# A hybrid transformer layer in split fp32: each stage's first pair of weights queued ahead of its last operands, and work moved between three engines

## Chip, cores and metric

The kernel runs on one core of one Trainium2 chip, in one launch. The metric is the device time of that launch in microseconds (us).

## What is computed

One layer on 1024 tokens of width 1024, all float32 (cut to what matters here):

```python
u = rmsnorm(h, g_mix_pre)
z = u @ w_in                          # 1024 x 4256; holds the two gates gate_a, gate_b
ya = (a_b * causal_dwconv3(a_c * a_x, conv_a_w)) @ w_a_out
yb = chunk_causal_attention(q, k, v) @ w_b_out
mixed = sigmoid(gate_a) * ya + sigmoid(gate_b) * yb
h = h + rmsnorm(mixed @ w_o, g_mix_post)
u2 = rmsnorm(h, g_ffn_pre)
up = causal_dwconv3(u2 @ w_ffn_up, conv_ffn_w) + b_ffn_conv    # width 2 x 2816
f = (gelu(up[:, :2816]) * up[:, 2816:]) @ w_ffn_down
h = h + rmsnorm(f, g_ffn_post)
h = h + rmsnorm((p @ w_ple_proj) * sigmoid(h @ w_ple_gate), g_ple_post)
```

## The kernel before

**Arithmetic.** Every fp32 operand is split into a high part (a cast on ScalarE, L181) and a low part (source minus high part, L182, on VectorE or GpSimd). A product is then three passes of matmuls. The large products are done on 2 x 2 blocks with seven block products in place of eight; one block product is 12 matmuls of 128x128 by 128x512 (`prod`, L300).

**Operands of a stage.** `x_blocks` turns eight activation tiles into seven operands: B11 and B21 (`first`), then B22, T2 and four wide subtractions of 128x2048 (`second`, L278), then T3, T1 and T4 (`third`). A `third` is released only once the last subtraction has been issued on VectorE.

**Weights.** `pair` turns two weight rows into two output rows. It loads both rows, forms S-combinations (two on GpSimd as a rule, L338 and L339; two on VectorE, L340 and L341), splits them, and runs the seven products. VectorE gathers them from PSUM (L348 to L363).

**First rows.** `first_row` does two of the seven products alone, those that need only B11 and B21. It runs for some pairs ahead of the stage, so that TensorE has work while the other operands are made. ScalarE copies the first product out of PSUM (L313), VectorE adds the second to it (L319); in the last stage GpSimd and VectorE add both to what is there (L316, L317). Such a pair is *early* and needs five products later.

**Order.** Each engine has an instruction queue that it works off in order. The queues' order is fixed when the kernel is built, by a scheduler that places instructions by modelled times; the source's order, tile buffers (rings of slots, `raws` for raw weight rows) and explicit `issue_after` edges bound it.

**Stages.** TensorE takes up new operands four times: at the gates (about 60 to 140 us into the span; 6 first rows), at the FFN's up projection (about 765 to 860 us; 12 first rows, with the layer's merge, its two norms and the residual add before it), and at two groups of the down projection (1200 to 1240 us and 1280 to 1340 us; 4 first rows each). In the merge, each half h computes a norm, eight residual adds (L845, L846), a second norm and the scaled activations (L852). A norm's sum over channels is made of squares (ScalarE, L247), summed on VectorE (L250), then by tiny matmuls with ones (L228) and transposes (L240) on TensorE. Between up and down the gated product of the FFN (`gated`: the convolution L513, gelu L891, a multiplication L892) goes to DRAM (`d_f`) and comes back as the operands of down.

## Time and profile before

| | us |
|---|---|
| median of 3 runs | 1546.74 (1546.2, 1546.74, 1549.32) |
| the profiled execution's own time | 1545.98 |
| its span in the trace | 1544.1 |
| TensorE busy in the span | 1476.6 (96%) |
| VectorE busy | 1174.8 (76%) |
| ScalarE busy | 689.0 (45%) |
| GpSimd busy | 545.0 (35%) |

The profile calls TensorE's matmuls PE, its weight loads PEld, VectorE DVE, ScalarE ACT, GpSimd POOL, and the queue that issues most DMAs SP. PEclk is the clock that TensorE was granted, as a share of full speed. Numbers after L are lines of the kernel before, where the text does not say otherwise.

### The profile page before, as it was taken

The page shows a single profiled execution, that of the slowest core. Times are in us where ns is not written, and L with a number is a line of the kernel's source. Part 1 is how long each engine was busy: PE and PEld are TensorE (multiplying, and loading weights), DVE is VectorE, ACT ScalarE, POOL GpSimd, SP SyncE. Part 2 cuts the span into 40 slices and gives each one's busy share as a digit, 9 for nine tenths or more (in the row PEclk, how much of TensorE's full clock was granted, in tenths as well). Part 3 has the DMA queues.
Part 4 walks back from the last instruction along what each step waited for, and adds up shares of the span by engine and source line. Part 5 has one row for each costly group of instructions (what it writes and reads, how often), then busy time and mean ns, then how long its engine had stood idle before and what let it go on. Part 6 is the DMA issues. An engine that isn't in the chain of part 4 may idle for free. (4 is left out here: it accounts for less than half of the span.)

```text
span 1544.1 us, 19277 instructions
## 1 busy us (share of the span) xinstructions
PE 1476.6 (96%) x6980; PEld 1225.9 (79%) x6980; DVE 1174.8 (76%) x1663; ACT 689.0 (45%) x1082; POOL 545.0 (35%) x402
## 2 busy tenths in 40 slices
PE   8999999999989999999998999999999699899996
PEld 6777888888778888888886888888888577688796
DVE  6897666665568888845579988889889878647876
ACT  8534222334457777343344444444446234135433
POOL 1333222226333343431033332223330214756963
PEclk9999999999999999999999999999999899999998
DMA  9344221336741013633271233334325523353332
GB/s 346 120 150 156 82 82 55 123 124 231 253 132 49 31 42 110 206 108 100 106 272 42 95 110 125 121 123 137 100 92 191 177 69 118 93 170 110 109 113 93
DMA packets 73503, 195.56 MB, mean 127 GB/s; under 512 B 7360, under 2 KB 22208, under 8 KB 73408
## 3 DMA queue, kind: packets, MB, share of 16 engines
q1 hardware_dynamic: 65056, 169.90, 33.6%
q10 hardware_dynamic: 8352, 24.44, 4.1%
q8 instruction: 55, 0.90, 0.2%
q14 instruction: 40, 0.33, 0.1%
HBM read 142.79 MB, written 51.51 MB: 126 GB/s over the span
## 5 line engine op out<-in xcount | busy, mean ns | idle before, releaser
L300 PE MATMUL psum<-s,s 128*128 128x512 f32 x3948 | 915.1, 393 | 32.7 <-DVE s L182 8.8
L300 PEld LDWEIGHTS psum<-s,s 128*128 128x128 f32 x3948 | 743.1, 189 | 199.6 <-DVE s L182 16.9
L181 ACT CAST s<-s 128x512 fp32r<-128x512 f32 (+3 forms) x431 | 340.1, 811 | 477.0 <-PE psum L300 157.6
L182 POOL TENSOR_TENSOR s<-s,s 128x512 fp32r<-128x512 f32 (+2 forms) x186 | 280.4, 1520 | 726.2 <-PE psum L300 423.7
L215 PE MATMUL psum<-s,s 128*128 128x512 f32 (+1 forms) x1920 | 413.4, 373 | 15.2 <-ACT s L181 13.5
L215 PEld LDWEIGHTS psum<-s,s 128*128 128x128 f32 x1920 | 335.6, 191 | 77.5 <-ACT s L181 15.5
L182 DVE TENSOR_TENSOR s<-s,s 128x1024 fp32r<-128x1024 f32 (+2 forms) x245 | 308.7, 1278 | 46.6 <-ACT s L181 44.2
L513 DVE SCALAR_TENSOR_TENSOR psum<-s,vecs,psum 128x1023 f32<-128x1023 f32 (+1 forms) x88 | 111.7, 1280 | 1.0
L250 DVE TENSOR_TENSOR s<-s,s 128x512 f32<-128x512 f32 (+1 forms) x83 | 65.9, 797 | 42.6 <-ACT s L247 40.6
L511 ACT ACTIVATE psum<-s,vecs 128x1024 f32<-128x1024 f32 x44 | 53.0, 1208 | 94.1 <-DVE s L359 80.6
L182 DVE TENSOR_TENSOR s<-psum,s 128x512 fp32r<-128x512 f32 (+3 forms) x144 | 70.8, 504 | 27.5 <-ACT s L181 26.3
L181 ACT CAST s<-psum 128x512 fp32r<-128x512 f32 (+3 forms) x144 | 61.2, 445 | 38.0 <-DVE s L182 13.9
L247 ACT ACTIVATE s<-s 128x512 f32<-128x512 f32 (+1 forms) x82 | 47.8, 590 | 52.8 <-DVE s L1004 21.3
L731 PE MATMUL psum<-s,s 128*128 128x512 f32 (+2 forms) x288 | 67.4, 360 | 2.3 <-ACT s L742 2.2
L338 POOL TENSOR_TENSOR s<-s 128x512 f32<-128x512 f32 x45 | 65.4, 1454 | 3.4
L339 POOL TENSOR_TENSOR s<-s,s 128x512 f32<-128x512 f32 x43 | 65.0, 1513 | 3.3
L744 POOL TENSOR_SCALAR s<-s,ri 128x384 f32<-128x384 f32 (+5 forms) x48 | 41.3, 861 | 70.3 <-DVE ri L743 52.8
L357 DVE TENSOR_TENSOR s<-s,psum 128x512 f32<-128x512 f32 x47 | 32.1, 683 | 34.0 <-PE psum L300 31.4
L756 PE MATMUL psum<-s,s 128*128 128x256 f32 x320 | 54.1, 292 | 1.5 <-DVE s L182 0.7
L731 PEld LDWEIGHTS psum<-s,s 128*128 128x128 f32 x288 | 46.4, 189 | 9.9 <-ACT s L742 5.3
L742 ACT ACTIVATE s<-psum,nm 128x128 f32<-128x128 f32 (+3 forms) x64 | 47.5, 745 | 14.3 <-DVE nm L740 8.9
L756 PEld LDWEIGHTS psum<-s,s 128*128 128x128 f32 x320 | 45.5, 189 | 6.0 <-DVE s L182 2.0
(115 smaller groups left out, 1067.2 us busy)
## 6 DMA issues: line engine op xcount, KB each, us to landing
s<-in_w_up_dram SPq DMA_DIRECT2D x56, 512.0 KB, 3.7
s<-in_w_in_dram SPq DMA_DIRECT2D x40, 512.0 KB, 3.8
s<-in_w_down_dram SPq DMA_DIRECT2D x36, 512.0 KB, 3.7
d_f<-s SPq DMA_DIRECT2D x22, 512.0 KB, 2.6
s<-in_x_dram SPq DMA_DIRECT2D x32, 256.0 KB, 5.4
d_sg<-s ACTq DMA_DIRECT2D x16, 512.0 KB, 3.1
s<-d_sg SPq DMA_DIRECT2D x16, 512.0 KB, 4.2
s<-d_f SPq DMA_DIRECT2D x16, 512.0 KB, 5.8
```

The lines of the kernel that those rows point to most:

```text
L181: A.copy(hi, src)
L182: (eng or V).tensor_sub(lo, src, f(hi))
L215: nc.tensor.matmul(out_ps, w[c // HALF][pw][:, c % HALF : c % HALF + P], X[k][half][px][:, cs], start=start and a == 0 and k == 0, stop=st ...
L247: A.activation(sq, src, AF.Square)
L250: V.tensor_add(acc, acc, sq)
L300: nc.tensor.matmul(pt, w[pw][:, k * P : (k + 1) * P], blk[k][px], start=a == 0 and k == 0, stop=a == 2 and k == 3,)
L338: who[2].tensor_add(a22, a21, a22)
L339: who[3].tensor_sub(a21, a11, a21)
L511: A.activation(dst, src, AF.Identity, bias=bias, scale=w2)
L513: V.scalar_tensor_tensor(dst[:, i:], src[:, : S - i], w, dst[:, i:], op0=ALU.mult, op1=ALU.add)
L731: nc.tensor.matmul(st_[:, lo_ : lo_ + w_], q[part_q][:, o : o + P], parts(K[hd, kh])[part_k][:, 0:w_], start=part_q == 0 and part_k == 0, ...
L756: nc.tensor.matmul(po[:, 0:256], vt[:, kt, :], t_[:, kk * 256 : (kk + 1) * 256], start=kt == 0 and part == 0, stop=kt == 2 * b + 1 and par ...
```

## The change

1. **First rows leave by ScalarE.** `first_row` copies the second product out of PSUM on ScalarE, where VectorE added it to the first. The sum of the two is made on GpSimd when the early pair starts.
2. **Weights apart from products.** The part of `pair` that loads and makes weights is now `weights`. At the gates, at up and at the first group of down, the weights of the first pair are issued ahead of `third`, and `third` waits for three things to be issued on VectorE: the last subtraction, T2 and the last split of those weights. In the second group of down they are issued ahead of `second`, and `third` does not wait for them. The rings of raw slots start at other slots, and have one slot more in the first group of down.
3. **Norm squares in PSUM.** In the merge the squares go to PSUM banks 5 and 6.
4. **Residual adds.** All 16 are on GpSimd (eight were).
5. **Down weights.** All on VectorE (18 operations were on GpSimd). The last group's low parts of the first half (6 splits) go from GpSimd to VectorE, and wait for the weights of the last two pairs.

```diff
     def square_sum(acc, src, accs, sqs):
-        sq = single(*(accs if acc is None else sqs)())[:, :n]
+        at = (accs if acc is None else sqs)()
+        sq = (single(*at) if isinstance(at, tuple) else bank(at))[:, :n]
...
         def second():
...
             operand("T2", 4, 1)
-            t4.append(sub(b21, b21, b22))
+            ends["sum"] = sub(b21, b21, b22)
-        def third():
-            with tc.issue_after(t4[0].ins):
+        def third(w=None):
+            with ExitStack() as after:
+                for i in (ends["sum"], ends["T2"], *([w["end"]] if w else [])):
+                    after.enter_context(tc.issue_after(i.ins))
                 operand("T3", 0, 1)
...
         if add:
-            G.tensor_add(d11, d11, m1)
             V.tensor_add(d11, d11, b2)
         else:
-            V.tensor_add(d11, b2, m1)
+            A.copy(d11, b2)
-    def pair(src0, src1, B, raws, banks, out0, out1, early=False, hooks=(), add=None, who=(V, G, G, G)):
+    def weights(src0, src1, raws, early=False, who=(V, G, G, G)):
...
+        w["S2"], w["S4"] = wide(r0, V)
+        w["S3"], w["S1"] = wide(r1, V)
+        w["end"] = last[-1]
+        return w
+    def pair(w, B, banks, out0, out1, hooks=(), add=None):
...
+        if "A11" in w:
+            A.copy(m1, times("A11", "B11"))
+            V.tensor_add(d11, times("A12", "B21"), m1)
+        else:
+            G.tensor_add(d11, d11, m1)
...
     second()
-    third()
+    w = gate_weights(spilled, True)
+    third(w)
...
-    sqs, accs, sqs2, accs2 = (Ring(singles(i)) for i in (46, 47, 48, 49))
+    sqs, accs, accs2 = Ring([5, 6]), Ring(singles(47)), Ring(singles(49))
-    sbk, rbk = Ring([4, 5, 6]), Ring([7])
+    sbk, rbk = Ring([4]), Ring([7])
...
-            (G if k % 2 else V).tensor_add(y, y, xr)
+            G.tensor_add(y, y, xr)
...
+    raws = Ring([42, 43, 7, 8])
+    mm = Ring(range(4))
+    w = up_weights(0)
     third()
-    raws = Ring([7, 8, 42, 43])
-    mm = Ring(range(4))
...
-        raws = Ring([7, 8] if g else [7, 8, 45])
+        raws = Ring([7, 8] if g else [7, 8, 45, 50])
...
+        def down_weights(i):
+            return weights(w_down[8 * g + 2 * i], w_down[8 * g + 2 * i + 1], raws, True, (V, V, V, V))
+        w = down_weights(0)
         second()
         if g == 0:
-            free = [50]
-            gated(*last)
-        third()
-        raws = Ring([7, 8, 22, 23] if g else [8, 45, 7, 50])
+            gated(*before, fo=before[2])
+        third(w if g == 0 else None)
+        raws = Ring([22, 23, 7, 8] if g else [45, 50, 7, 8])
...
-            split(raw, *fX[k][h], V if h else G)
+            with tc.issue_after(ends[2 + h]):
+                split(raw, *fX[k][h], V)
```

**VectorE's queue at the entry to up**, from the scaled activations of the second half on. In these rows sN is a tile in slot N; slots 7, 8, 42 and 43 hold raw weight rows, 34 to 41 the activations, 17, 21, 25, 29 and the split at 38 receive operands (T2 at 21 is made from 34; T3 and T1 at 25 and 29 from 38; T4 at 38 from 34), 0, 3 and 50 receive split weights. In the changed kernel L182 is L183, L278 is L281, L340 and L341 are L338 and L339, and L852 is L869. Before:

```order
L852 SCALAR_TENSOR_TENSOR s34_102<-s34_102,vecs_70,psum_69 128x512 x4
L278 TENSOR_TENSOR s38_2471<-s38_2471 128x4x512
L319 TENSOR_TENSOR s33_5883<-psum_69,s33_5883 128x512
L340 TENSOR_TENSOR s7_88<-s8_89,s7_88 128x512
L182 TENSOR_TENSOR s17_539<-s34_102,s17_539 128x2x512 x2
L278 TENSOR_TENSOR s38_2471<-s34_102,s38_2471 128x4x512
L319 TENSOR_TENSOR s46_4960<-psum_69,s46_4960 128x512
L341 TENSOR_TENSOR s7_88<-s7_88 128x512
L182 TENSOR_TENSOR s0_124<-s8_89,s6_422 128x1024
L278 TENSOR_TENSOR s34_102<-s34_102,s38_2471 128x4x512
L319 TENSOR_TENSOR s47_4961<-psum_69,s47_4961 128x512
L182 TENSOR_TENSOR s50_5853<-s7_88,s45_5852 128x1024
```

And now:

```order
L869 SCALAR_TENSOR_TENSOR s34_102<-s34_102,vecs_70,psum_69 128x512 x4
L183 TENSOR_TENSOR s2_134<-s7_88,s1_127 128x1024
L281 TENSOR_TENSOR s38_2477<-s38_2477 128x4x512
L183 TENSOR_TENSOR s17_539<-s34_102,s17_539 128x2x512 x2
L281 TENSOR_TENSOR s38_2477<-s34_102,s38_2477 128x4x512
L281 TENSOR_TENSOR s34_102<-s34_102,s38_2477 128x4x512
L338 TENSOR_TENSOR s42_4890<-s43_4891,s42_4890 128x512
L281 TENSOR_TENSOR s34_102<-s34_102 128x4x512
L339 TENSOR_TENSOR s42_4890<-s42_4890 128x512
L183 TENSOR_TENSOR s21_119<-s34_102,s21_119 128x2x512 x2
L183 TENSOR_TENSOR s25_564<-s38_2477,s25_564 128x2x512 x2
L183 TENSOR_TENSOR s29_569<-s38_2477,s29_569 128x2x512 x2
```

The three L319 adds are gone from between the subtractions. Behind the rows shown the queue now has the two weight splits (s0, s50) and the last operand (s38, two splits). Before, it had two operands (s25, s29), a gathering add, the operand at 21, the second pair's L340 and the last operand.

**VectorE's queue at the first group of down.** Slots 9 to 16 hold the activations, 45 and 50 raw weight rows, 34 and 49 outputs of first rows; T2 goes to slot 38, T3 to 17, T1 to 42, 43, 33 and 44. In the changed kernel L513 is L530, L892 is L914, and the GpSimd or VectorE weights L338 and L339 are L336 and L337. Before:

```order
L278 TENSOR_TENSOR s13_8423<-s13_8423 128x4x512
L182 TENSOR_TENSOR s17_539<-s9_8418,s17_539 128x2x512 x2
L182 TENSOR_TENSOR s42_8577<-s9_8418,s42_8577 128x512
L182 TENSOR_TENSOR s43_8578<-s9_8418,s43_8578 128x512
L182 TENSOR_TENSOR s33_8579<-s9_8418,s33_8579 128x512
L182 TENSOR_TENSOR s44_8580<-s9_8418,s44_8580 128x512
L182 TENSOR_TENSOR s38_6218<-s13_8423,s38_6218 128x2x512 x2
L513 SCALAR_TENSOR_TENSOR psum_69<-s48_4996,vecs_70,psum_69 128x1022
L338 TENSOR_TENSOR s45_8416<-s45_8416 128x512
L319 TENSOR_TENSOR s34_102<-psum_69,s34_102 128x512
L319 TENSOR_TENSOR s49_4997<-psum_69,s49_4997 128x512
```

And now:

```order
L281 TENSOR_TENSOR s13_8441<-s13_8441 128x4x512
L183 TENSOR_TENSOR s38_6238<-s13_8441,s38_6238 128x2x512
L530 SCALAR_TENSOR_TENSOR psum_69<-s48_5002,vecs_70,psum_69 128x1022
L183 TENSOR_TENSOR s38_6238<-s13_8441,s38_6238 128x2x512
L337 TENSOR_TENSOR s8_89<-s7_88,s8_89 128x512
L183 TENSOR_TENSOR s5_4885<-s50_8435,s5_4885 128x512
L914 TENSOR_TENSOR s46_4966<-s46_4966,psum_69 128x1024
L338 TENSOR_TENSOR s7_88<-s8_89,s7_88 128x512
L336 TENSOR_TENSOR s50_8435<-s50_8435 128x512
L183 TENSOR_TENSOR s4_389<-s8_89,s3_137 128x1024
L183 TENSOR_TENSOR s17_539<-s9_8436,s17_539 128x2x512 x2
```

The adds that emptied two first rows' banks stood behind eight operand splits and a convolution; now no such add is in the queue, and T2 is split first, and the first pair's weights (raw slots 7 and 8) stand ahead of the splits of T3 and T1.

**GpSimd's queue in the merge.** The residual adds of one half; the last weights of the merge stand ahead. Slots 42 and 43 hold the halves of x. Before:

```order
L182 TENSOR_TENSOR s33_356<-s7_88,s33_356 128x512
L846 TENSOR_TENSOR s38_2471<-s38_2471,s42_4884 128x512
L846 TENSOR_TENSOR s38_2471<-s38_2471,s43_4885 128x512
L846 TENSOR_TENSOR s34_102<-s34_102,s42_4884 128x512
L846 TENSOR_TENSOR s34_102<-s34_102,s43_4885 128x512
```

And now:

```order
L183 TENSOR_TENSOR s33_356<-s7_88,s33_356 128x512
L863 TENSOR_TENSOR s38_2477<-s38_2477,s42_4890 128x512 x2
L863 TENSOR_TENSOR s38_2477<-s38_2477,s43_4891 128x512 x2
L863 TENSOR_TENSOR s34_102<-s34_102,s42_4890 128x512 x2
L863 TENSOR_TENSOR s34_102<-s34_102,s43_4891 128x512 x2
```

Four adds of a half became eight in a row on the same engine.

## Rows read from the trace of the kernel before

**Rows 1.** The page's head: busy time, share of the span and count of instructions of TensorE (with its weight loads), VectorE, ScalarE and GpSimd.

```profile
PE 1476.6 (96%) x6980; PEld 1225.9 (79%) x6980; DVE 1174.8 (76%) x1663; ACT 689.0 (45%) x1082; POOL 545.0 (35%) x402
```

**Rows 2.** Windows by stage (gates, entry to up, rest of up, down's first group, down's second group, what follows): start and end, then their length, busy us (and instructions) of PE, PEld, DVE, ACT, POOL, the granted clock, the DMA share and GB/s.

```profile
60.00:140.00 80.00, 74.88 (x316) 58.12 (x315) 71.79 (x102) 37.37 (x49) 29.57 (x17) 1.00 0.39 134
820.00:860.00 40.00, 34.65 (x133) 25.31 (x132) 38.17 (x35) 14.82 (x17) 19.52 (x10) 0.91 0.16 53
860.00:1180.00 320.00, 320.00 (x1413) 265.15 (x1413) 287.38 (x312) 139.08 (x143) 92.47 (x63) 1.00 0.37 123
1200.00:1240.00 40.00, 27.56 (x102) 20.99 (x102) 35.68 (x37) 12.09 (x13) 11.48 (x6) 0.87 0.47 166
1280.00:1340.00 60.00, 50.21 (x209) 39.68 (x209) 48.27 (x42) 18.09 (x25) 36.33 (x24) 0.94 0.40 123
1340.00:1400.00 60.00, 60.00 (x267) 49.68 (x266) 34.52 (x47) 20.65 (x34) 35.81 (x27) 1.00 0.43 140
```

**Rows 3.** Waits over the whole span: engine, tile and line that waited, what it waited for, total us, times, longest us.

```profile
PE psum L300 <- DVE s L182: 8.8, 12, 1.8
PE psum L300 <- DVE s L319: 6.7, 1, 6.7
PE psum L300 <- DVE s L350: 6.4, 1, 6.4
PE psum L300 <- DVE s L349: 6.1, 2, 5.2
...
DVE s L340 <- POOL s L339: 18.7, 14, 4.4
```

**Rows 4.** Instructions by source line: count, then shortest, median and longest duration in ns, first and last start.

```profile
L278 DVE TENSOR_TENSOR s<-s x8: 2282/2292/3384, 56.4 to 1280.9; 128x2048 f32<-128x2048 f32 x8
...
L340 DVE TENSOR_TENSOR s<-s,s x45: 677/685/1780, 55.8 to 1324.4; 128x512 f32<-128x512 f32 x45
...
L319 DVE TENSOR_TENSOR s<-psum,s x22: 682/688/698, 46.0 to 1210.6; 128x512 f32<-128x512 f32 x22
...
L313 ACT COPY s<-psum x26: 567/586/592, 43.4 to 1299.0; 128x512 f32<-128x512 f32 x26
...
L339 POOL TENSOR_TENSOR s<-s,s x43: 1274/1294/3219, 50.1 to 1322.1; 128x512 f32<-128x512 f32 x43
...
L846 POOL TENSOR_TENSOR s<-s,s x8: 1285/1300/3589, 720.0 to 782.2; 128x512 f32<-128x512 f32 x8
```

**Rows 5.** Timeline at the gates, first PE, then VectorE: start, length, engine, line, operation, count, and in brackets idle time before it and what ended it.

```profile
54.81 19.20 PE L300 MATMUL psum<-s,s 128*128 128x512 f32 x84
74.83 0.73 PE L300 MATMUL psum<-s,s 128*128 128x512 f32 x2 [0.82 <-ACT s L181]
...
72.79 0.69 DVE L340 TENSOR_TENSOR s<-s,s 128x512 f32<-128x512 f32 x1 [1.18 <-POOL s L339]
```

**Rows 6.** Timeline at the entry to up, PE, then VectorE.

```profile
804.58 25.43 PE L300 MATMUL psum<-s,s 128*128 128x512 f32 x111
830.45 0.73 PE L300 MATMUL psum<-s,s 128*128 128x512 f32 x2 [0.43 <-DVE s L182]
...
841.72 8.52 PE L300 MATMUL psum<-s,s 128*128 128x512 f32 x24 [1.49 <-DVE s L182]
...
804.86 5.35 DVE L852 SCALAR_TENSOR_TENSOR s<-s,vecs,psum 128x512 f32<-128x512 f32 x8 [1.73 <-PE psum L240]
...
824.79 3.37 DVE L278 TENSOR_TENSOR s<-s 128x2048 f32<-128x2048 f32 x1
828.09 5.71 DVE L182 TENSOR_TENSOR s<-s,s 128x1024 fp32r<-128x1024 f32 x4
```

**Rows 7.** Timeline of the second half's two norms, PE between the first norm's transposes (at 771.07) and the second norm's sum, then GpSimd's residual adds.

```profile
771.42 24.07 PE L300 MATMUL psum<-s,s 128*128 128x512 f32 x105
795.34 0.95 PE L228 MATMUL psum<-ones,s 128*128 128x1 f32 x8
...
773.65 2.60 POOL L846 TENSOR_TENSOR s<-s,s 128x512 f32<-128x512 f32 x2 [43.81 <-DVE s L845]
779.52 4.92 POOL L846 TENSOR_TENSOR s<-s,s 128x512 f32<-128x512 f32 x2 [3.27 <-DMA s<-in_x_dram]
```

**Rows 8.** Timeline at down's first group: PE, VectorE, ScalarE.

```profile
1211.42 13.13 PE L300 MATMUL psum<-s,s 128*128 128x512 f32 x48 [6.67 <-DVE s L319]
1229.76 7.33 PE L300 MATMUL psum<-s,s 128*128 128x512 f32 x24 [5.22 <-DVE s L349]
...
1201.23 7.04 DVE L182 TENSOR_TENSOR s<-s,s 128x1024 fp32r<-128x1024 f32 x8
1208.18 1.29 DVE L513 SCALAR_TENSOR_TENSOR psum<-s,vecs,psum 128x1022 f32<-128x1022 f32 x1
...
1209.97 1.30 DVE L319 TENSOR_TENSOR s<-psum,s 128x512 f32<-128x512 f32 x2
...
1217.50 2.00 ACT L181 CAST s<-s 128x1024 fp32r<-128x1024 f32 x2 [2.28 <-DMA s<-d_f]
```

**Rows 9.** Timeline at down's second group: PE, then VectorE.

```profile
1321.57 15.45 PE L300 MATMUL psum<-s,s 128*128 128x512 f32 x60 [6.44 <-DVE s L350]
...
1313.32 1.76 DVE L340 TENSOR_TENSOR s<-s 128x512 f32<-128x512 f32 x1 [2.43 <-POOL s L339]
...
1320.82 0.69 DVE L350 TENSOR_TENSOR s<-psum,s 128x512 f32<-128x512 f32 x1
```

More of the change, by code (lines that the diff above doesn't have):

```diff
@@ L341, in pair, with times @@
         V.tensor_sub(a12, a12, a11)
[L342 to L343 removed]
+        w["S2"], w["S4"] = wide(r0, V)
[3 more added lines that the diff above has]
+    def pair(w, B, banks, out0, out1, hooks=(), add=None):
+        d11, d12, d21, d22 = out0[:, hs(0)], out0[:, hs(1)], out1[:, hs(0)], out1[:, hs(1)]
+        def times(a, b):
+            pt = bank(banks())
+            prod(pt, w[a], B[b])
+            return pt
         m1, u3 = (d12, d21) if add is None else add
         u2 = m1
[L346 to L350 removed]
+        if "A11" in w:
[3 more added lines that the diff above has]
+            G.tensor_add(d11, d11, m1)
+        V.tensor_add(u2, times("S2", "T2"), m1)
+        V.tensor_add(u3, times("S3", "T3"), u2)
         if add is not None:
@@ L353, in pair @@
                 G.tensor_add(d, d, u_)
-        pt = times(S1, "T1")
+        pt = times("S1", "T1")
         for hook in hooks[:1]:
@@ L358, in pair @@
         V.tensor_add(d12, d12, pt)
-        V.tensor_add(d21, d21, times(A22, "T4"))
-        pt = times(S4, "B22")
+        V.tensor_add(d21, d21, times("A22", "T4"))
+        pt = times("S4", "B22")
         for hook in hooks[1:]:
@@ L430, with gate_weights, gate_pair @@
     wblk.become([*range(NBLK), 33, 50])
-    def gate_pair(i, o, o2, early=False, hooks=()):
-        pair(w_in[17 + 2 * i], w_in[18 + 2 * i], B, raws, mm, f32(o), f32(o2), early, hooks)
+    def gate_weights(i, early=False):
+        return weights(w_in[17 + 2 * i], w_in[18 + 2 * i], raws, early)
+    def gate_pair(i, o, o2, early=False, hooks=(), w=None):
+        pair(w or gate_weights(i, early), B, mm, f32(o), f32(o2), hooks)
         for j, o_ in enumerate((o, o2)):
@@ L519 @@
             ct = 2 * g + j
-            pair(w_in[4 + ct], w_in[8 + ct], B, raws, mm, v, e)
+            pair(weights(w_in[4 + ct], w_in[8 + ct], raws), B, mm, v, e)
             V.tensor_mul(v, v, e)
@@ L524 @@
             rotary_tables()
-        pair(w_in[2 * g], w_in[2 * g + 1], B, raws, mm, v, e)
+        pair(weights(w_in[2 * g], w_in[2 * g + 1], raws), B, mm, v, e)
         for j, z in ((1, e), (0, v)):
@@ L537 @@
             w1 = w_in[12 + k1] if k1 < 5 else w_in[33]
-            pair(w_in[12 + k0], w1, B, raws, mm, f32(o[0]), f32(o[1]))
+            pair(weights(w_in[12 + k0], w1, raws), B, mm, f32(o[0]), f32(o[1]))
             for k, o_ in zip((k0, k1), o):
@@ L880, in up, with gated @@
         z1 = free.pop(0)
-        pair(w_up[j], w_up[NFF + j], B, raws, mm, f32(z0), f32(z1), j in early or j in spilled, who=(G, G, G, G))
+        pair(w, B, mm, f32(z0), f32(z1))
         return j, z0, z1
-    def gated(j, z0, z1):
+    def gated(j, z0, z1, fo=None):
         cv = []
@@ L894, in gated @@
         free.extend([z0, z1, fo])
-    last = up(0)
+    before = up(0, w)
     for j in range(1, NFF):
-        now = up(j)
-        gated(*last)
-        last = now
+        now = up(j, up_weights(j))
+        gated(*before)
+        before = now
     raws = Ring([7, 8])
@@ L906 @@
     free = [i for i in free if i not in extra]
-    yacc = [i for two in zip(free[:4], [*free[4:], *last[1:]]) for i in two]
+    yacc = [i for two in zip(free[:4], [*free[4:], *before[1:]]) for i in two]
     extra = [42, 43, *extra]
```

46 lines of the change are left out of this document (20 added, 26 removed).

## The prediction

> **What bounds the kernel now.** I read the page's head first: TensorE is busy 96% of the span, every other engine far less [rows 1]. So time can only be won where TensorE stands or runs slowly. The windows by stage show where. In the long part of up TensorE never stands: 1413 matmuls in 320 us, 0.2265 us each [rows 2]. With that as yardstick, each stage's window minus its matmuls at 0.2265 is what the stage loses: gates 80 − 316 × 0.2265 = 8.4 us; entry to up 40 − 133 × 0.2265 = 9.9; down's first group 40 − 102 × 0.2265 = 16.9; its second group 60 − 209 × 0.2265 = 12.7. Together 47.9 us. Part of this is standing, part a lower granted clock: 0.91, 0.87 and 0.94 as window means, where 1.00 (2.4 GHz) stands in the windows in which TensorE never stood. So a stall that goes also gives back the slow stretch behind it, and I count whole losses.
>
> What TensorE waits for is VectorE: the longest single waits are 6.7 us for a first-row add, 6.4 for a gathering add, and 6.1 in two pieces for another [rows 3]. These are queueing delays: the add takes 0.69 us [rows 4] but stands behind other work on VectorE. VectorE in turn waits 18.7 us in all for GpSimd's weight combinations.
>
> **The change, term by term.**
>
> *Gates (loses 8.4).* Six first-row adds leave VectorE: 6 × 0.6 us pitch (0.688 each, overlapping) = 3.6 us less in the train of operands behind which TensorE stands in pieces [rows 5]. ScalarE takes six copies of 0.586 [rows 4]; it is busy 37 of 80 us there [rows 2], so they hide. But GpSimd gets six adds, at about the 1.29 us of its combinations, and the same VectorE instruction reads 2.29 us as a rule and 3.38 at most, or 0.685 and 1.78 [rows 4]: 1.09 longer in both when GpSimd is at work beside it. If each of the six hits one, that is 6.5 us back. Bounds −3.6 to +2.9; I take −1, since the adds come one per pair and most land later in the stage. The Trainium skill has a rule against this part: in "SBUF — State Buffer", section "Who interferes with whom", VectorE and GpSimd share one pair of ports as an exclusive lock, and a VectorE operation with two SBUF inputs contends with a GpSimd one that reads SBUF, so that the loser stops fully. By it, each add could cost its whole 1.29 us, 7.7 for six, and the term would be +4.1 and the sum 5 us worse. The rows agree with whom it hits: L319, one input of which lies in PSUM, never took over 0.698.
>
> *Entry to up (loses 9.9).* TensorE runs 111 matmuls from 804.58 and is dry at 830.01; then it takes two matmuls at a time as each split comes out, until 841.72 [rows 6]. In the new order 50 more first-row matmuls stand behind the second norm's transposes (137 where there were 87), so it is dry at 804.6 + 161 × 0.2265 = 841. VectorE's train from 804.9 is 5.35 us of scaled activations, four subtractions at 2.2 (8.8), 2.3 for B22, 1.2 for two combinations, six splits at about 1.14 (6.9) and the weights' 2 × 1.14: 27 us, so it ends at 832 plus 1.2 for a leftover split; T4 takes 2.3 more. Contention adds 1.09 for each of some four GpSimd operations: 837 to 840. So the stall would go entirely, 9.9. Against it: those 50 matmuls are missing ahead. Between the first norm's transposes and the second norm's sum TensorE had 105 matmuls, 24.07 us [rows 7]; now 82, 18.6 us. In that time eight adds run in a row on GpSimd: 8 × 1.30 = 10.4 [rows 4], ahead of them 0.7 and 1.5 us, behind them a square and a sum, 1.3; and the wait for x, 3.27 before [rows 7]: 17.2. It just fits, with 1.4 us to spare; I take 2 us of standing there, and 2 at the entry. Gain 6, bounds 4 to 10.
>
> *Down's first group (loses 16.9).* The 6.67 wait is two L319 adds at 1209.97, behind 7.04 us of operand splits and a 1.29 us convolution [rows 8]. Now no such add is in VectorE's queue; ScalarE empties the banks with a 0.59 us copy. The 6.67 goes. The 5.22 wait at L349 comes behind weight work and splits that wait for ScalarE. The first pair's weights now stand ahead of T3 and T1, so its products can start; what is late next is ScalarE's chain: casts there waited 2.28 us for operands from DRAM [rows 8]. I leave about 9 us in small waits (casts, combinations, splits one behind the other, 1 to 2.6 each). Gain 8, bounds 3 (only half of the 6.67) to 12 (both waits, 11.9).
>
> *Down's second group (loses 12.7).* TensorE stands 6.44 us for an L350 at 1320.82; before it VectorE stood 2.43 us for GpSimd's L339 and ran its own combinations at 1.76 instead of 0.69 [rows 9]. With all down weights on VectorE the wait goes and so does the stretching: 2.43 + about 3 stretches of 1.09, which with the slow clock behind covers most of it. Gain 8, bounds 6 to 12.
>
> *Edits at nothing.* The 18 combinations on VectorE are 18 × 0.6 = 11 us, the six last splits 3.6; behind 1340 VectorE is busy 34.5 of 60 us [rows 2]. If that room were not there, they would be waited for by TensorE at 0.6 each. In the long part of up, 12 GpSimd adds could stretch VectorE by 12 × 1.09 = 13 us; it has 320 − 287 = 33 idle. ScalarE's copies, 22 × 0.586 = 13 us and those of the down groups, hide in an engine 45% busy [rows 1]. Squares in PSUM change no duration that a row shows; they take one SBUF input from VectorE's sum.
>
> *Sum:* −1 − 6 − 8 − 8 = −23 us on the profiled execution's 1545.98: 1523. The median stands 0.76 above that execution: 1524.
>
> **The rivals.**
>
> 1. *GpSimd's added adds lengthen the trains.* Gates at +3, up −3, the groups −6 and −7: −13, 1534. For it: L339 and L846 themselves reach 3.2 and 3.6 us [rows 4], signs of collisions. Against it: in the down groups the change takes GpSimd work away. The rule quoted from the Trainium skill at the gates leads the same way. Chance 0.15.
> 2. *Down's first group keeps its stall.* The wait for VectorE becomes one for ScalarE's casts, which wait for operands from DRAM and for the gelu: gain 2 instead of 8, 1530. For it: the 2.28 us wait in the rows, and a cast now ahead of which the weights stand. Against: the raw weights come in early. Chance 0.09.
> 3. *Slower: TensorE stands at the second norm's sum.* Eight adds in a row take 8d, with 2.0 to 3.5 us around them, against 18.6 us of matmuls in the second half and about the same in the first. At the median d of 1.30 it fits. From d = 2.0 TensorE stands; at the longest add, 3.59, the chain is 8 × 3.59 + 2.3 = 31 us, and TensorE stands 12.4 us in each half, 25 us. With the other terms at their low ends (gates +3, up 0, groups −3 and −6: −6) that gives 1546 + 19 = 1565; with them at my values but up at 0, 1546 − 17 + 25 = 1554. It decides from d of about 2.7 at the low ends (2 × (21.6 + 2.3 − 18.6) = 11 against 6), and from 3.3 at my values. Against it: the sums and the scalings, VectorE's work in that time, have an input in PSUM now, the kind that no row shows stretched, and six of the eight adds were short. Chance 0.09, 1554.
> 4. *It all works.* The losses of the four stages shrink to gates 6, up 0, groups 4 and 2: 36 us less, 1511. Chance 0.06.
> 5. *The change does not do what it says.* The queues' order is made from modelled times; on the chip the moved work could be ready no earlier, and gains and new stands cancel: 1546. Chance 0.06.
>
> **How the numbers follow.** The forecast, 1524, has 0.55 with its own range of 1515 to 1531. From 1510 to 1543 the range takes in rivals 1, 2 and most of 4, and leaves out 3, 5 and the rest: about 0.17. Faster by over 0.2% (3.1 us, about what a measurement of this kernel can tell from no change) is the forecast and rivals 1, 2 and 4, 0.85; within it rival 5, 0.06; slower rival 3, 0.09.
>
> **What would show it.** In the changed profile: no wait of TensorE on a first-row operation in down's first group, and waits there under 3 us each; no 6 us wait on the second pair's gathering add in the second group; at the entry to up TensorE running from the transposes for about 36 us before its first wait; at the gates about as many matmuls in 80 us as now; between the two norms of the merge a stand of at most 2 us before the sum. The prediction is wrong if the residual adds take over 2 us each and TensorE waits for the sum, if the waits on ScalarE in down's first group add up to what VectorE's did, or if VectorE's subtractions mostly read 3.4 us.

## The result and the profile after

The changed kernel takes 1537.48 us (median of 4 runs, 1536.82 to 1538.62) against 1546.47 for the kernel before beside it: ratio 0.9939, 95% interval 0.9922 to 0.9956, so 9 us faster. The forecast was 1524, 22 us faster, with a range of 1510 to 1543. The way was right; less than half of the gain came.

The page's head and the windows by stage of the changed kernel, columns as in [rows 1] and [rows 2]:

```profile
PE 1476.9 (96%) x6980; PEld 1228.5 (80%) x6980; DVE 1175.3 (76%) x1657; ACT 699.8 (46%) x1104; POOL 550.7 (36%) x408
```

```profile
60.00:140.00 80.00, 73.52 (x301) 57.79 (x300) 73.88 (x94) 33.87 (x46) 33.99 (x21) 0.94 0.37 124
820.00:860.00 40.00, 31.55 (x128) 25.38 (x127) 36.09 (x31) 12.77 (x15) 18.97 (x11) 0.87 0.16 53
860.00:1180.00 320.00, 320.00 (x1414) 264.96 (x1413) 285.86 (x312) 137.57 (x140) 107.27 (x73) 1.00 0.36 117
1200.00:1240.00 40.00, 34.08 (x131) 25.90 (x130) 37.63 (x40) 14.87 (x18) 5.35 (x4) 0.91 0.48 171
1280.00:1340.00 60.00, 57.37 (x250) 46.14 (x249) 55.71 (x62) 18.49 (x24) 23.67 (x15) 1.00 0.40 118
```

Against [rows 2] TensorE did more matmuls in both groups of down (131 for 102, 250 for 209) and fewer at the gates (301 for 316) and at the entry to up (128 for 133). The added GpSimd work shows at the gates, 33.99 us for 29.57, and VectorE is not relieved there: 73.88 for 71.79.

Both kernels issue the same 6980 matmuls. So the count that TensorE has done up to a time at which both are in the same stage says how far one is ahead, at 0.222 us a matmul (90 in 20 us). TensorE alone, in stretches of the changed kernel's trace:

```profile
0.00:150.00 150.00, 136.45 (x575) 0.97 0.55 192
150.00:660.00 510.00, 497.32 (x2522) 1.00 0.36 117
660.00:900.00 240.00, 231.55 (x1032) 0.98 0.35 118
900.00:1250.00 350.00, 344.08 (x1498) 0.99 0.40 133
1250.00:1350.00 100.00, 96.38 (x420) 1.00 0.37 108
```

The same stretches of the kernel before hold 590, 2523, 1038, 1470 and 386 matmuls.

| stretch | gates | to 660 | merge and up | down, first group | down, second group | behind 1350 |
|---|---|---|---|---|---|---|
| forecast, us | −1 | 0 | −6 | −8 | −8 | 0 |
| measured, matmuls ahead | −15 | −1 | −6 | +28 | +34 | −6 |
| measured, us | +3.3 | +0.2 | +1.3 | −6.2 | −7.6 | +1.4 |

Up to 1350 us the changed kernel is 40 matmuls or 8.9 us ahead, and the spans differ by 7.5 (1536.6 and 1544.1); the last column is what lies between the two and no count of its own. It fits a slower clock near 1430: 31 matmuls take 10.23 us there and 8.75 before, at a granted clock of 0.79 against 0.89 in the 16 us around them. What lowers it there was not looked into.

At the gates, GpSimd's adds (L361) stand in the middle of VectorE's train of operands. Timeline of GpSimd, VectorE and TensorE, and then the window in which TensorE stood:

```profile
51.89 1.30 POOL L361 TENSOR_TENSOR s<-s 128x512 f32<-128x512 f32 x1 [0.94 <-ACT s L324]
59.07 1.43 POOL L361 TENSOR_TENSOR s<-s 128x512 f32<-128x512 f32 x1 [5.88 <-ACT s L324]
...
65.47 2.27 POOL L361 TENSOR_TENSOR s<-s 128x512 f32<-128x512 f32 x1
...
73.95 1.52 POOL L361 TENSOR_TENSOR s<-s 128x512 f32<-128x512 f32 x1 [2.90 <-ACT s L324]
...
59.27 3.38 DVE L281 TENSOR_TENSOR s<-s,s 128x2048 f32<-128x2048 f32 x1
62.58 1.77 DVE L339 TENSOR_TENSOR s<-s 128x512 f32<-128x512 f32 x1
...
87.42 14.91 PE L306 MATMUL psum<-s,s 128*128 128x512 f32 x52 [1.16 <-DVE s L362]
```

```profile
80.00:100.00 20.00, 15.61 (x50) 11.29 (x50) 16.64 (x19) 6.82 (x8) 5.97 (x3) 0.74 0.16 57
```

The subtraction takes 3.38 us instead of 2.29 and the combination 1.77 instead of 0.69 [rows 4], beside an add that neither VectorE nor TensorE waits for. TensorE's stands between 74 and 88 us are as many as in the kernel before but longer: six of 0.40 to 1.61 us, 6.4 in all, against six of 0.21 to 0.82, 2.6 in all. The granted clock falls to 0.74 as the mean of a window (80 to 100 us) that held 1.00 before, and 52 matmuls take 14.91 us, 0.287 each.

At the entry to up, TensorE, then VectorE, then GpSimd:

```profile
797.14 33.23 PE L306 MATMUL psum<-s,s 128*128 128x512 f32 x145
838.82 11.51 PE L306 MATMUL psum<-s,s 128*128 128x512 f32 x38 [8.45 <-DVE s L183]
...
798.36 5.35 DVE L869 SCALAR_TENSOR_TENSOR s<-s,vecs,psum 128x512 f32<-128x512 f32 x8
...
809.24 5.58 DVE L281 TENSOR_TENSOR s<-s,s 128x2048 f32<-128x2048 f32 x2
820.86 1.78 DVE L338 TENSOR_TENSOR s<-s,s 128x512 f32<-128x512 f32 x1 [6.05 <-POOL s L337]
...
826.46 15.71 DVE L183 TENSOR_TENSOR s<-s,s 128x1024 fp32r<-128x1024 f32 x10
...
806.02 11.06 POOL L183 TENSOR_TENSOR s<-s,s 128x512 fp32r<-128x512 f32 x2 [20.17 <-PE psum L306]
...
828.70 2.38 POOL L183 TENSOR_TENSOR s<-s,s 128x512 fp32r<-128x512 f32 x1 [4.91 <-ACT s L182]
831.03 2.24 POOL L361 TENSOR_TENSOR s<-s 128x512 f32<-128x512 f32 x1
833.24 2.24 POOL L336 TENSOR_TENSOR s<-s 128x512 f32<-128x512 f32 x1
835.55 2.13 POOL L337 TENSOR_TENSOR s<-s,s 128x512 f32<-128x512 f32 x1
```

Against [rows 6] the many short stands became one of 8.45 us. GpSimd's two low parts of the first pair took 11.06 us; VectorE stood 6.05 us for the combination behind them; then its ten splits took 15.71 us, 1.57 each, where such splits follow each other at 1.14. Of the four GpSimd instructions beside these ten splits only one (831.03) is a first-row add; the others make the second pair's weights.

In the merge, TensorE reached the second norm's sum without a stand, and the sixteen residual adds have the median of the eight of before [rows 4] and a shorter longest one (timeline of TensorE, then the adds by source line, shortest, median and longest ns):

```profile
771.01 18.86 PE L306 MATMUL psum<-s,s 128*128 128x512 f32 x82
789.71 0.95 PE L230 MATMUL psum<-ones,s 128*128 128x1 f32 x8
```

```profile
L863 POOL TENSOR_TENSOR s<-s,s x16: 1287/1300/1861, 723.2 to 784.6; 128x512 f32<-128x512 f32 x16
```

In down, the waits of [rows 8] and [rows 9] (6.67, 5.22 and 6.44 us) are gone. What is left is at most 3.85 us, for a cast of ScalarE in the first group; in the second group no wait is over 1.2 us. The first and one of the second:

```profile
1213.67 8.18 PE L306 MATMUL psum<-s,s 128*128 128x512 f32 x24 [3.85 <-ACT s L182]
...
1312.44 19.35 PE L306 MATMUL psum<-s,s 128*128 128x512 f32 x84 [0.58 <-DVE s L363]
```

### The profile page after: what moved, and what is told of

Read it like the earlier page. It is cut to its first block, busy times and chain, and to the rows that moved or that the text cites. A ratio compares the mean times of both kernels' runs of the same rounds, so it can differ in the third digit from the quotient of the medians.

```text
span 1536.6 us, 19320 instructions
## 1 busy us (share of the span) xinstructions
PE 1476.9 (96%) x6980; PEld 1228.5 (80%) x6980; DVE 1175.3 (76%) x1657; ACT 699.8 (46%) x1104; POOL 550.7 (36%) x408
## 5 line engine op out<-in xcount | busy, mean ns | idle before, releaser
L306 PEld LDWEIGHTS psum<-s,s 128*128 128x128 f32 x3948 | 744.9, 189 | 188.3 <-DVE s L183 18.9
L182 ACT CAST s<-s 128x512 fp32r<-128x512 f32 (+3 forms) x431 | 339.7, 811 | 424.0 <-PE psum L306 129.8
L183 POOL TENSOR_TENSOR s<-s,s 128x512 fp32r<-128x512 f32 (+2 forms) x174 | 263.7, 1528 | 544.7 <-PE psum L306 355.7
L217 PEld LDWEIGHTS psum<-s,s 128*128 128x128 f32 x1920 | 335.7, 191 | 77.2 <-ACT s L182 14.9
L183 DVE TENSOR_TENSOR s<-s,s 128x1024 fp32r<-128x1024 f32 (+2 forms) x257 | 318.2, 1257 | 53.2 <-ACT s L182 43.6
L530 DVE SCALAR_TENSOR_TENSOR psum<-s,vecs,psum 128x1023 f32<-128x1023 f32 (+1 forms) x88 | 111.7, 1279 | 1.0
L183 DVE TENSOR_TENSOR s<-psum,s 128x512 fp32r<-128x512 f32 (+3 forms) x144 | 70.8, 504 | 27.6 <-ACT s L182 26.6
L182 ACT CAST s<-psum 128x512 fp32r<-128x512 f32 (+3 forms) x144 | 61.2, 445 | 37.9 <-DVE s L183 13.8
L361 POOL TENSOR_TENSOR s<-s 128x512 f32<-128x512 f32 x22 | 32.2, 1466 | 123.0 <-ACT s L324 57.2
L250 ACT ACTIVATE s<-s 128x512 f32<-128x512 f32 (+1 forms) x68 | 39.0, 581 | 46.8 <-DVE s L1034 23.4
L337 POOL TENSOR_TENSOR s<-s,s 128x512 f32<-128x512 f32 x39 | 57.6, 1477 | 2.9
L336 POOL TENSOR_TENSOR s<-s 128x512 f32<-128x512 f32 x39 | 54.9, 1408 | 2.9
L253 DVE TENSOR_TENSOR s<-s,s 128x512 f32<-128x512 f32 (+1 forms) x55 | 45.6, 829 | 12.1 <-ACT s L250 11.0
L748 PEld LDWEIGHTS psum<-s,s 128*128 128x128 f32 x288 | 46.4, 189 | 9.9 <-ACT s L759 5.3
L759 ACT ACTIVATE s<-psum,nm 128x128 f32<-128x128 f32 (+3 forms) x64 | 47.6, 746 | 14.3 <-DVE nm L757 9.0
```

The source lines that it names most:

```text
L182: A.copy(hi, src)
L183: last.append((eng or V).tensor_sub(lo, src, f(hi)))
L217: nc.tensor.matmul(out_ps, w[c // HALF][pw][:, c % HALF : c % HALF + P], X[k][half][px][:, cs], start=start and a == 0 and k == 0, stop=st ...
L253: V.tensor_add(acc, acc, sq)
L306: nc.tensor.matmul(pt, w[pw][:, k * P : (k + 1) * P], blk[k][px], start=a == 0 and k == 0, stop=a == 2 and k == 3,)
L336: who[2].tensor_add(a22, a21, a22)
```

## Experiments

**Theory R** (A in the first expectations): GpSimd's adds at the pairs' start, new work beside VectorE's trains, ate the gain at gates and up. **Rivals**: B, the new order itself is the harm; S, which came up after the first four runs, GpSimd is held up because VectorE's trains lost the instructions that read PSUM. Diffs are against the changed kernel unless said otherwise; us are medians, and the kernel before took 1546.7 to 1548.7 beside them. In the columns behind the ratio stand matmuls ahead of the kernel before, by the stretches used above; the runs ending in _merge have the merge as before the change in addition:

| run | us | ratio, 95% | gates | to 660 | up | down 1 | down 2 |
|---|---|---|---|---|---|---|---|
| whole change | 1537.48 | 0.9922 to 0.9956 | −15 | −1 | −6 | 28 | 34 |
| first_v | 1525.64 | 0.9845 to 0.9878 | −4 | 8 | 10 | 33 | 42 |
| upfirst_v | 1533.70 | 0.9897 to 0.9924 | −7 | 7 | 4 | 28 | 34 |
| gates_old | 1536.15 | 0.9911 to 0.9938 | −13 | 2 | −8 | 29 | 34 |
| down_alone | 1531.88 | 0.9891 to 0.9918 | 3 | 5 | −2 | 29 | 31 |
| copy_v | 1539.60 | 0.9928 to 0.9954 | −23 | 2 | −2 | 20 | 35 |
| add_v | 1525.65 | 0.9845 to 0.9879 | 15 | 11 | 13 | 28 | 32 |
| first_upv | 1527.80 | 0.9858 to 0.9885 | 1 | −3 | 6 | 29 | 43 |
| first_gold | 1527.88 | 0.9854 to 0.9881 | 1 | −4 | 14 | 29 | 42 |
| down_w_g | 1540.42 | 0.9939 to 0.9966 | −14 | 2 | −9 | 22 | 19 |
| d0_old | 1538.06 | 0.9926 to 0.9951 | −13 | 7 | 7 | 21 | 32 |
| merge_old | 1530.31 | 0.9873 to 0.9900 | −8 | 8 | 15 | 29 | 35 |
| best_a | 1530.52 | 0.9875 to 0.9902 | −6 | 0 | 25 | 29 | 23 |
| add_v_merge | 1526.46 | 0.9855 to 0.9888 | 14 | 6 | 14 | 32 | 32 |
| adds_twice | 1551.79 | 1.0020 to 1.0042 | −28 | −1 | −27 | 13 | 24 |
| part1_alone | 1537.40 | 0.9927 to 0.9952 | −2 | 12 | 9 | 5 | 15 |
| first_merge | 1525.33 | 0.9842 to 0.9874 | 2 | 0 | 16 | 28 | 42 |
| mixed | 1522.91 | 0.9830 to 0.9857 | 3 | 11 | 13 | 32 | 42 |
| mixed_merge | 1523.44 | 0.9834 to 0.9865 | 12 | 8 | 14 | 33 | 42 |

Counts come from one profiled execution each. gates_old turned out to have every queue in the same order as the whole change, so it tests nothing; its counts are within 3 matmuls by stage, its median within 1.3 us. The counts repeat less well than that. Up to 660 us the whole change, gates_old, upfirst_v, merge_old, down_w_g and d0_old have the same work in the same order on TensorE, VectorE and GpSimd, yet they are 7 to 15 matmuls behind at the gates and 0 to 16 behind at 660 us; and add_v, add_v_merge, mixed and mixed_merge, alike up to there too, are 3 to 15 ahead at the gates. So up to 12 matmuls at the gates, and 16 by 660 us (3.6 us), mean nothing by themselves. The counts at up and down repeat better: in down's second group 31 to 35 in nine runs that have one add at the pairs' start and all of part 5 (only best_a has 23, which nothing here explains), and 42 or 43 in the six whose first rows leave there as before the change.

**first_v**, part 1 undone:

```diff
         if add:
+            G.tensor_add(d11, d11, m1)
             V.tensor_add(d11, d11, b2)
         else:
-            A.copy(d11, b2)
+            V.tensor_add(d11, b2, m1)
...
-        else:
-            G.tensor_add(d11, d11, m1)
```

> Part 1 of the change undone: first rows leave by a VectorE add again, GpSimd has no add at a pair's start; the rest of the change stays. Theory A (GpSimd work laid into VectorE's operand trains is what ate the gain at gates and up: VectorE loses about 1.1 us for each GpSimd instruction beside it, and GpSimd itself is held up): at the gates TensorE is fewer matmuls behind the kernel before at 150 us than the change's 15, at most 8; the slow-clock stretch there shortens; at up VectorE still waits 4 us or more for GpSimd's combinations of the first pair, since they stay on GpSimd; down's first group gives back 2 to 6 us; sum 1535 to 1541. Rival B (the new order, weights ahead of the last operands, is itself the harm, GpSimd is incidental): 15 matmuls behind at the gates as with the whole change, sum 1540 to 1544.

1525.64: far below both. A part of the change that was to win time costs 12 us in the company of the others. Rival B falls: with the new order kept, the gates are 4 matmuls behind. Theory A was wrong in two places: down's first group gives back nothing, and VectorE no longer waits for GpSimd's combinations at the entry to up.

**upfirst_v**, `(G, G, G, G)` at up is `(V, V, V, V)` for the first pair:

> The whole change, but at up the first pair's weights (two combinations, three low parts) are made on VectorE instead of GpSimd. Theory A: the 6.05 us for which VectorE waited for GpSimd's combination is gone, VectorE gets about 3 us of work more; TensorE's wait of 8.45 us at the entry to up falls to 4 to 5 and the slow clock behind it shortens; 1531 to 1534. Rival B (what delays TensorE is that the weights' split stands behind six operand splits in VectorE's queue): the wait grows by the 3 us that VectorE got more, 1538 to 1541.

1533.70, within theory A's range, and TensorE's wait fell to 5.38 us, a little more than its 4 to 5. But of the 26 matmuls that this execution is ahead of the whole change's at 1350 us, 16 come before 660, where the queues are the same; only 10 come at up. Beside VectorE's train, which then ran from 804.80 to 825.86 without a gap, one of GpSimd's adds took 22.84 us. Instructions by source line (shortest, median, longest ns) and VectorE's train:

```profile
L361 POOL TENSOR_TENSOR s<-s x22: 1251/1292/22842, 51.5 to 1205.0; 128x512 f32<-128x512 f32 x22
```

```profile
817.22 6.89 DVE L183 TENSOR_TENSOR s<-s,s 128x1024 fp32r<-128x1024 f32 x6
824.03 0.68 DVE L339 TENSOR_TENSOR s<-s 128x512 f32<-128x512 f32 x1
```

VectorE's six splits ran at 1.15 us each: while GpSimd was held here, VectorE lost nothing. This suggested S.

**gates_old**, `third()` ahead of the first pair's weights at the gates:

> The whole change, but at the gates the first pair's weights are issued behind the last operands again; first rows still leave by ScalarE and are added on GpSimd. Theory A: GpSimd's adds are the larger part of the loss at the gates, so at 150 us TensorE is still 8 to 15 matmuls behind the kernel before; 1536 to 1538. Rival B: the order is the loss, so at 150 us it is within 4 matmuls of the kernel before; 1534.

1536.15; the same order came out, as told above.

**down_alone**, gates, merge and up as before the change:

> Gates, merge and up as before the change, the two groups of down and what follows as changed. If the stages' gains are independent, the 6.2 and 7.6 us of the down groups come without the losses of gates and up: 1546.5 - 13.8 = 1533, or 1534 if the 1.4 us of slower clock in the last part comes too. If the down groups' gain hangs on what gates and up do: 1537 as with the whole change, or more.

1531.88. The down groups' gain stands by itself. The gates, the merge and the entry to up, as changed, cost 5.6 us.

**copy_v** and **add_v** tell S from R: one puts PSUM reads back into the trains and leaves GpSimd its adds, the other takes the adds away and puts none back.

```diff
-            A.copy(d11, b2)
+            V.tensor_copy(d11, b2)        # copy_v
...
-            G.tensor_add(d11, d11, m1)
+            V.tensor_add(d11, d11, m1)    # add_v
```

> The whole change, but the copy of a first row's second product is made by VectorE instead of ScalarE; GpSimd still adds the two products at the pair's start. Theory S (starvation: a GpSimd instruction that meets a train of VectorE instructions with both inputs in SBUF gets on only in openings, and VectorE's instructions with an input in PSUM are such openings; the change took the first-row adds, which read PSUM, out of the trains): the openings are back, no GpSimd instruction at the entry to up takes over 4 us, VectorE's wait for GpSimd there is under 2 us; 1526 to 1531, although VectorE has 22 copies more and GpSimd keeps its 22 adds. Rival R (the number of GpSimd instructions beside VectorE's trains is what costs): as the whole change or slower, 1537 to 1540.

> The whole change, but the add of the two first-row products at the pair's start is on VectorE (both inputs in SBUF) instead of GpSimd; ScalarE still copies. Theory S: VectorE's trains still have no opening, so GpSimd's low parts and combinations of the first pair at up still take 4 us or more each and VectorE waits for them; 1531 to 1538. Rival R: GpSimd's adds are gone, so is their cost; 1524 to 1527.

1539.60 and 1525.65: S falls as the cause of the 12 us, R stands for the changed kernel. In copy_v nothing on GpSimd at the entry to up took over 4 us and VectorE did not wait for it, as S asks, and the kernel was still no faster than the whole change; its seven splits took 12.35 us, 1.76 each. That GpSimd's low parts were short again (3.67 us for two) is no proof of openings: they started at 807.17, beside the scaled activations, and were done before the first copy between the subtractions. In add_v the low parts were held up and VectorE waited for them, yet its splits ran undisturbed, and 15 matmuls behind at the gates became 15 ahead (over the runs with the same queues there, 7 to 15 behind and 3 to 15 ahead). With first_v the four cases are complete: without GpSimd's adds 1525.6, with VectorE's PSUM reads (first_v) or without (add_v); with the adds 1539.6 (copy_v) and 1537.5 (whole change). GpSimd and VectorE of copy_v, then of add_v:

```profile
807.17 3.67 POOL L183 TENSOR_TENSOR s<-s,s 128x512 fp32r<-128x512 f32 x2 [18.48 <-PE psum L306]
...
804.53 5.36 DVE L869 SCALAR_TENSOR_TENSOR s<-s,vecs,psum 128x512 f32<-128x512 f32 x8 [0.72 <-PE psum L242]
```

```profile
796.97 9.74 POOL L183 TENSOR_TENSOR s<-s,s 128x512 fp32r<-128x512 f32 x2 [19.69 <-PE psum L306]
...
818.35 8.75 POOL L183 TENSOR_TENSOR s<-s,s 128x512 fp32r<-128x512 f32 x1 [9.02 <-ACT s L182]
...
809.36 0.69 DVE L338 TENSOR_TENSOR s<-s,s 128x512 f32<-128x512 f32 x1 [6.15 <-POOL s L337]
...
815.57 8.03 DVE L183 TENSOR_TENSOR s<-s,s 128x1024 fp32r<-128x1024 f32 x7
```

Seven splits in 8.03 us, 1.15 each, against 1.57 with the adds. The adds do not explain this by their own length: in the changed kernel the second pair's low part got on beside the splits in 2.38 us and the splits lost; here it was held for 8.75 us and they lost nothing.

**adds_twice** doubles the suspected cost:

```diff
             G.tensor_add(d11, d11, m1)
+            G.tensor_add(d11, d11, m1)
```

> The whole change, with GpSimd's add at an early pair's start made twice: the first product is then counted twice in the first half of the first rows' blocks, so the output is another. Theory R (GpSimd's adds beside VectorE's trains are the cost; 26 of them cost 11.8 us, by the run that moved them to VectorE): as many again cost 6 to 12 us more, 1543 to 1550. If what counts is only where the first pair's weights fall in GpSimd's queue: they come later by at most three adds at each entry, 1538 to 1542.

1551.79, just above the range: 14.3 us more for 26 more adds. The loss falls at gates, up and down alike. VectorE's ten splits at up now take 1.89 us each and TensorE stands 10.95 us behind them:

```profile
847.09 15.24 PE L306 MATMUL psum<-s,s 128*128 128x512 f32 x57 [10.95 <-DVE s L183]
...
831.51 18.93 DVE L183 TENSOR_TENSOR s<-s,s 128x1024 fp32r<-128x1024 f32 x10
```

**down_w_g** and **d0_old** look for the source of the gain in down:

```diff
-            return weights(..., raws, True, (V, V, V, V))
+            return weights(..., raws, True, (V, G, G, G) if i else (V, V, V, V))   # down_w_g
...
-        third(w if g == 0 else None)
+        third()                                                                    # d0_old
+        if g == 0:
+            w = down_weights(0)
```

> The whole change, but the down weights of the second to fourth pair have their low parts and two combinations on GpSimd again, as before the change (part 5 undone, the last group's splits apart). If part 5 is what won down's second group: between 1250 and 1350 us TensorE gains 10 matmuls or fewer on the kernel before, where the whole change gained 34, and the time is 1541 to 1545. If the earlier weights of the first pair won it: 25 or more, 1537 to 1539.

> The whole change, but in down's first group the first pair's weights are issued behind the last operands again, as before the change; first rows still leave by ScalarE. If the order won the first group: between 900 and 1250 us TensorE gains 12 matmuls or fewer on the kernel before, where the whole change gained 28; 1541 to 1544. If ScalarE's copies won it (the prediction's reason: no first-row add behind VectorE's splits): 20 or more, 1537 to 1539.

down_w_g (1540.42, 19 matmuls) lies between its two cases. d0_old (1538.06, 21 matmuls) falls on its second, the one that credits ScalarE's copies; but first_v, without the copies, has 33 matmuls there, and part1_alone below, with little else, 5. By these counts part 5 makes 15 of the second group's 34 matmuls and 6 of the first's 28; the order of the first group makes 7 of its 28. (d0_old's queue on VectorE also came out in another order at the entry to up, where it is 13 matmuls better, so its total says little.)

**part1_alone**, part 1 put into the kernel before:

> The kernel before with part 1 of the change alone: ScalarE copies a first row's second product, GpSimd adds the products at the pair's start; order, merge and down weights as before. Theory R: slower than the kernel before at gates and up by 3 to 8 us, less what down's first group wins by the missing first-row adds (0 to 6): 1546 to 1553. If part 1 helps where the prediction put it (down's first group, 6.7 us) and costs nothing else: 1540 to 1542.

1537.40: a miss of both, and of theory R as a general rule: the same adds do no harm in the old order. Alone, part 1 wins 9 us. It costs next to nothing at the gates, is 12 matmuls ahead from there to 660 us (no more than counts vary there), and wins 9 at up and 15 in down's second group; the first group of down, where the forecast put its whole gain, gets 5 matmuls of 28. The stalls there moved to ScalarE's casts, splits and gathering adds:

```profile
1204.49 3.87 PE L300 MATMUL psum<-s,s 128*128 128x512 f32 x8 [3.90 <-ACT s L181]
1209.16 2.36 PE L300 MATMUL psum<-s,s 128*128 128x512 f32 x4 [0.80 <-DVE s L182]
1213.10 10.22 PE L300 MATMUL psum<-s,s 128*128 128x512 f32 x36 [1.59 <-ACT s L181]
1225.32 5.76 PE L300 MATMUL psum<-s,s 128*128 128x512 f32 x24 [2.00 <-DVE s L350]
```

**merge_old**, parts 3 and 4 undone, and **first_merge**, parts 1, 3 and 4 undone:

> The whole change, but eight of the sixteen residual adds are on VectorE again and the norm's squares lie in SBUF (parts 3 and 4 undone). TensorE stood nowhere between the two norms in either trace, so theory R (GpSimd's adds at the pairs' start are the cost) expects the whole change's time within 2 us: 1535.5 to 1539.5. If the residual adds on GpSimd cost at the entry to up: 1533 or less.

> First rows by a VectorE add as before the change and the merge as before; of the change only the order of the weights and the down weights on VectorE remain. If the merge's part of the change costs by itself: 1518 to 1521. If it costs only together with GpSimd's adds at the pairs' start: 1524 to 1527.

1530.31, which is not what theory R expects but the second case, a cost of the merge's part; and 1525.33, as without part 1 alone. With the add on VectorE and the merge undone (add_v_merge) it was 1526.46. So the merge's part costs 7 us in the median, and only while GpSimd's adds are there. Of the 39 matmuls that merge_old's execution is ahead of the whole change's, 21 come at up, which is 4.7 us, and 16 before 660 us, where the queues are the same. At the entry to up, with the merge as before, VectorE's train begins at 801.5 instead of 798.4, and GpSimd's two low parts, at 802.34, take 3.65 us and are done before the subtractions, beside scaled activations that read PSUM; TensorE then stands 4.00 us instead of 8.45.

```profile
802.34 3.65 POOL L183 TENSOR_TENSOR s<-s,s 128x512 fp32r<-128x512 f32 x2 [17.81 <-ACT s L319]
...
832.87 29.32 PE L306 MATMUL psum<-s,s 128*128 128x512 f32 x117 [4.00 <-DVE s L183]
```

**Towards a better version.** first_upv is first_v and upfirst_v together, first_gold is first_v with the gates' old order, best_a is add_v with the first weights of gates and up on VectorE (`who` as in upfirst_v, for one pair at the gates and two at up).

> First rows by a VectorE add as before the change, and at up the first pair's weights all on VectorE; the rest as changed. Both theories: nothing in VectorE's train at up waits for GpSimd; the 4.29 us that TensorE waited at the entry to up in the run without the weights' move falls to 1 to 3; 1522 to 1525. If VectorE's 3 us of added work count in full: 7 us of wait, 1528.

> First rows by a VectorE add as before the change, and the order at the gates as before (weights of the first pair behind the last operands); the rest as changed. The gates are then the kernel before's, so at 150 us TensorE is within 3 matmuls of it, where the run with the new order was 5 behind; 1523 to 1525. If the new order at the gates helps later: 1526 or more.

> The add of the two first-row products on VectorE, and the weights of the first pair of the gates and of the first two pairs of up on VectorE too, so that hardly a GpSimd instruction stands beside the entries' trains; the rest as changed. Theory R: the 6.2 and 3.9 us that VectorE waited for GpSimd's combinations at up in the run with the add alone go, for some 5 us of work; 1520 to 1523. If VectorE's added work counts in full: 1526 to 1528.

1527.80, 1527.88 and 1530.52: the first two fall on their second case, the third misses both. With GpSimd's adds gone, nothing more is won by taking GpSimd's weights out of the trains, or by the old order; best_a, which theory R put lowest, is 4.9 us slower than add_v. **mixed** takes the best choice of each stage: add_v at gates and up, first rows as before the change in down.

> At the gates and up ScalarE copies the first rows' second product and VectorE makes the add at the pair's start (as in the run that moved the adds to VectorE); in the two down groups first rows leave by VectorE and GpSimd as before the change; the rest as changed. By the matmul counts the first choice is best at gates and up (14 and 14 matmuls ahead), the second in down's second group (43 against 32): 11 matmuls of 0.222 us less than with the add on VectorE everywhere, 1522 to 1524. If the stages' gains are not independent: 1525 to 1527.

1522.91, ratio 0.9843 (0.9830 to 0.9857), 14.6 us faster than the whole change, as expected in the sum. In its parts the gates gave 3 matmuls and not 14, and down's second group 42 as forecast. Its interval overlaps that of add_v, so the 2.7 us between the two are not certain. With the merge undone too (mixed_merge) it was 1523.44.

## Why the prediction was wrong

**The bound** was right: TensorE never stood in the long part of up (1414 matmuls, as before), and the edits priced at nothing cost nothing there.

**Gates, −1, measured +3.3.** The step that failed is "I take −1, since the adds come one per pair and most land later in the stage". Four of the six adds ran as soon as their copies were made, at 51.9, 59.1, 65.5 and 74.0 us, not at their pairs' start; only two came later, at 103.8 and 121.5. The upper bound priced the collisions rightly, six adds at 1.09 us or 6.5 us: between the six executions with these queues at the gates (7 to 15 matmuls behind) and the four with the adds on VectorE (3 to 15 ahead) lie 23 matmuls in the mean, 5 us. The value was chosen within the range without looking where GpSimd's queue had the adds.

**Entry to up, −6, measured +1.3.** Two steps failed. That TensorE is "dry at 804.6 + 161 × 0.2265 = 841" counted the 50 moved first-row matmuls as added and left the transposes at 804.2; the matmuls were missing ahead of them, the transposes came at 796.8, and TensorE ran dry at 830.4, as before. VectorE's train began 6.5 us sooner, which is all that the move could give. And "Contention adds 1.09 for each of some four GpSimd operations" priced only VectorE's side. From 798.4 the train would have needed about 28 us without contention (an estimate from its rows' undisturbed lengths), to about 826, and the split that TensorE waited for ended near 838.8: 12 us more, of which 6.05 are VectorE's wait for a GpSimd that was itself held up and the rest stretched instructions. The end at 837 to 840 was met by accident. The 2 us of standing between the two norms did not come; parts 3 and 4 cost 7 us in the median all the same (merge_old), with GpSimd's adds there. In the changed kernel the train starts 7.7 us ahead of GpSimd's low parts (798.4 and 806.0), with the merge as before 0.8 us ahead of them (801.5 and 802.3).

**Down's first group, −8, measured −6.2.** The size was right by luck, since the reason was wrong: ScalarE's copies, which were to win it, win 5 matmuls alone, and without them the group gains 33. The weights' place and engine account for 13 of the 28 by the runs that undo each (one execution each); how the rest divides was not separated.

**Down's second group, −8, measured −7.6.** The size was right, and part 5, to which the prediction gave the gain, makes 15 of the 34 matmuls; what makes the other 19 was not separated. Part 1 costs 8 there (42 without it). In this group ScalarE copies nothing for it: VectorE adds the second product as before, and only GpSimd's four adds move to the pairs' start.

**The rivals.** The first, GpSimd's added adds lengthening the trains, is what happened in the changed kernel, and at 1534 it was nearest; it too left out VectorE's wait for a GpSimd that is held up. The second did not come: the waits on ScalarE that took the place of VectorE's are 3.85 us at most, though the prediction's sign was "under 3 us each". The third, a stand at the second norm's sum, did not come: the adds' median was 1.30 us, and the wait is not in the trace. The doubled adds cost 14.3 us for 26, 0.55 us each over all places, so some collided and some did not. By the rule of the Trainium skill that was quoted, in "SBUF — State Buffer", section "Who interferes with whom", each add costs up to its own length. The trace agrees with it on who loses time: VectorE's combinations, with both inputs in SBUF, reach 1.78 us beside GpSimd, and none of its 415 adds of 128x512 with an input in PSUM took over 0.70 in the changed kernel.

**Open:** why part 1 wins 9 us in the kernel before and costs 12 in the changed one. Some of it hangs on the merge: with the merge as before, the adds cost 4 to 5 us (1530.31 against 1526.46 and 1525.33), and GpSimd's first low parts started beside the scaled activations, as in part1_alone, and not beside the subtractions. What decides the rest, and which engine loses where they meet, no run separated.

## What to carry to other kernels

Work given to an engine that is 35% busy is not free if that engine shares a resource with the one whose train bounds a stage: look where the queue puts the moved instruction, and price both engines' loss. When filler is moved from one side of a point to the other, the time at which it runs out stays (830.4 us here, 830.0 before); only the start of the work behind the point moves. A gain per stage, counted in matmuls done, shows what a total of several changes hides: here 62 matmuls won in down and 21 lost at gates and up. Count more than one execution, though: with the same queues the gates alone differed by up to 12.

## What the hardware did that was not expected

A GpSimd add that takes 1.29 us as a rule took 22.84 us in upfirst_v, beside 21 us of VectorE instructions that followed each other without a gap and had all their inputs in SBUF; the two low parts of up's first pair took 11.06 us in the changed kernel and 9.74 in add_v, beside such instructions too. The Trainium skill's page "SBUF — State Buffer" (section "Who interferes with whom") has the loser stop for the other's whole instruction; the trace shows it stopped for a whole train of them.

Not every such train holds GpSimd off. The ten splits of the changed kernel also follow each other without a gap, with all inputs in SBUF, and beside them four GpSimd instructions took 2.13 to 2.38 us each and VectorE lost 1.1 us at one split after another. What decides which of the two happens is not shown. Where the low parts started beside the scaled activations, which read PSUM, they took 3.67 us (copy_v) and 3.65 (merge_old), and then it was VectorE that lost: three of the four subtractions of copy_v took 3.2 to 3.4 us.
